# Issuing four follow-up steps of a two-layer gated trunk later in the instruction order

## The chip, the cores and the metric

The kernel runs on 1 core of one Trainium2 chip. The metric is device time in microseconds of one execution of the whole program.

## What is computed

Two layers of a block with two branches over 512 frames of width 1024, in float32. The reference, cut to what the change touches:

```python
for i in range(DEPTH):                                   # 2 layers
    proj = rmsnorm(x, norm1_g[i]) @ w_in[i]
    u_pool, q, k, v, g_a, g_b = split(proj)
    q = apply_partial_rotary(rmsnorm(q, q_norm_g[i]), cos, sin)
    k = apply_partial_rotary(rmsnorm(k, k_norm_g[i]), cos, sin)
    o = diff_attention(q, k, v, lam)                     # 4 heads, two softmaxes each
    attn_out = rmsnorm(o, subln_g[i]) * (1.0 - lam_init)
    pool_out = pool_mixer(u_pool, pool_w[i], pool_scale[i])   # windowed means less u, then a matmul
    merged = sigmoid(g_a) * pool_out + sigmoid(g_b) * attn_out
    x = x + merged @ w_out[i]
    x = x + swiglu(rmsnorm(x, norm2_g[i]))               # hidden width 2816
```

The rotation touches the first 32 of the 128 columns of each q and k. The pool mixer subtracts u from its mean over the last 2, 4, 8 or 16 frames, one window for each of four groups of 256 columns.

## The kernel before

**Products.** Every operand of a matmul is split into a high part, rounded to the matmul's type, and a low part, the rest (`split`, L216: ScalarE writes the high part, VectorE the low one). Each product is then three matmuls: high by high, high by low and low by high. One step of `product` (L302 to L314) is three matmuls of up to 512 columns each, 1536 columns in all.

**Heads.** A layer goes through its four heads in the order 3, 2, 1, 0 (`ORDER`). For head j, `attention` first projects q and k of four token tiles of 128 frames, eight steps each. `evicted` (L625) reads a finished tile out of PSUM: squares and their sums on ScalarE (L629), mean and power on VectorE and POOL (`rsqrt_mean`, L355 and L356). `normed` (L632) scales the tile by the result (four L634 on ScalarE), rotates it (`rotate`: three products L385 and a sum L393 on VectorE), and calls `turned`. That transposes 32 by 32 blocks on VectorE (L326), writes them to DRAM and reads them back in another order (L327 and four L331, issued by SP). In the first head of layer 0 TensorE transposes instead. `turn` then splits the result into qh and ql; `scores` multiplies, takes the row maximum (L550) and the exponential (L551); `joined` combines the two softmaxes; `turn_prob` splits the probabilities (ah, al); `weighted` multiplies by v and `gated` scales the result (L599); `turn_out` writes it into `mj`.

**Branches of the head before.** Between the projections of q and k and that of v, `between` calls `branches` for the head before. It makes two products for the pool mixer, each followed by `windowed` (L697), and two for the gates, each followed by a product with the rows of 1/rms (L731) and a tanh (L732). `windowed` scales the sums (L702), adds up 1 to 4 times with growing shifts (L707), subtracts u (L711, L713) and rounds the result into uh and ul (`split` in L714). `merged` later multiplies uh and ul by the pool weights and merges with the gates and `mj`.

**The order of issue.** The program is unrolled. A counter `clock` adds up the columns of the matmuls issued so far. `later(delay, what)` puts a piece of work on a heap, due that many columns on; `after` does the same, or runs it at once for a delay of 0. `run_due`, called ahead of every step of a product, issues all that is due. `need` issues what is on the heap, in order of due time, until the keys that it is given are in `ready`. From this order of issue the framework builds a queue for each engine. `NORMED` (4800) is the delay from `evicted` to `normed`, `QK_AWAY` (28000) that from `evicted` to `turn`.

**Buffers.** Tiles with one tag share a ring. The ring "qn" has three buffers and holds the tiles of `evicted` and their transposed copies; "us" has two, used by `windowed`; "ta" (the gates) two; the PSUM ring "mm" six and "sc" (scores) two.

Of the kernel before, what the change touches and what calls it, by code (L numbers as in the profile page):

```python
# [13 lines left out]
AF = mybir.ActivationFunctionType  # L14
# [8 lines left out]
NT = S // P  # L23
# [30 lines left out]
SCORE_WAIT, PROB_WAIT, AV_WAIT, NORM_WAIT, MERGE_WAIT = 33600, 25200, 11400, 15000, 15000  # L54

QK_AWAY, SCORE_AWAY, PROB_AWAY, AV_AWAY, MERGE_AWAY = 28000, 26000, 32000, 18000, 24000
NORMED, JOINED, GATED = 4800, 2400, 4800
HIDDEN_DELAYS = (26000, 28000), (8000, 14000)


# [64 lines left out]
def trunk_kernel(  # L125
# [10 lines left out]
    nc = tc.nc  # L136
# [5 lines left out]
    def mm_ps():  # L142
        return ps.tile([P, 512], F32, name="mm", tag="mm", bufs=6)
# [10 lines left out]
    scale = const.tile([P, 3 * L * KD + 4 * L], F32, name="scale")  # L154
# [20 lines left out]
    def gain_column(layer, i):  # L175
        k = 3 * L * KD + 4 * layer + i
        return scale[:, k:k + 1]
# [36 lines left out]
    def split(hi, lo, src):  # L214

        return nc.scalar.copy(hi, src), nc.vector.tensor_sub(lo, src, hi.bitcast(F32))  # L216
# [37 lines left out]
    def wblock(n):  # L254

        return [pair for _ in range(n // 2) for pair in piece()]
# [7 lines left out]
    def later(delay, what):  # L264
        heapq.heappush(waiting, (clock[0] + delay, count[0], what))
        count[0] += 1

    def after(delay, what):
        if delay:
            later(delay, what)  # L270
        else:
            what()

    def run_due(done=None):

        if running[0]:
            return
        running[0] = True
        while waiting and (waiting[0][0] <= clock[0] if done is None else not done()):
            heapq.heappop(waiting)[2]()  # L280
        running[0] = False
        assert done is None or done()
# [34 lines left out]
    def transpose(dst, src):  # L317
        nc.tensor.transpose(dst, src, ident)
        clock[0] += 2 * P
# [25 lines left out]
    def squares_of(x):  # L345
        return x.rearrange("p k (q j) -> p k q j", q=4)

    def rsqrt_mean(ss, n, width, times=(1.0,), eps=None):

        r = sb.tile([P, width], F32, name="r", tag="r", bufs=4)  # L350
        part = width // len(times)
        for i, f in enumerate(times):
            cs = slice(i * part, (i + 1) * part)
            e = EPS / (f * f) if eps is None else eps[i]
            nc.vector.tensor_scalar(r[:, cs], ss[:, cs], 1.0 / (n * f * f), e, op0=ALU.mult, op1=ALU.add)  # L355
        nc.gpsimd.tensor_tensor(r, r, mhalf[:, :width], op=ALU.pow)  # L356
        return r

    def small(name, width=1):
        return sb.tile([P, width], F32, name=name, tag=name, bufs=4)  # L360

    ready = set()

    def need(*keys):
        run_due(lambda: all(k in ready for k in keys))
# [9 lines left out]
    def pair(name, tag, n):  # L375
        return [sb.tile([P, n, S], F32R, name=name + part, tag=tag, bufs=2) for part in "hl"]

    def rotate(qn, t, layer):

        cs, sn = rotary[layer]  # L380
        both = sb.tile([P, 4, 4, ROT], F32, name="m12", tag="m12")

        def by(to, x, table):
            to, x = (v.rearrange("p (a h) r -> p a h r", a=2) for v in (to, x))
            nc.vector.tensor_mul(to, x, table.unsqueeze(2).broadcast_to(list(x.shape)))  # L385

        m1, m2 = both[:, 0], both[:, 1]
        by(m1, qn[:, :, :ROT], cs[:, :, t, :])
        for a in range(2):
            b = (1 - a) * HALF  # L390
            here = slice(a * HALF, (a + 1) * HALF)
            by(m2[:, :, here], qn[:, :, b:b + HALF], sn[:, :, t, here])
        nc.vector.tensor_add(qn[:, :, :ROT], m1, m2)  # L393

    def token(t):
        return slice(t * P, (t + 1) * P)
# [102 lines left out]
    for layer in range(L):  # L499
# [14 lines left out]
        def attention(j, before, then, between):  # L514
# [3 lines left out]
            at_start = not layer and j == ORDER[0]  # L518
# [3 lines left out]
            mj = sb.tile([P, 2, S], F32, name="mj", tag="mj", bufs=2)  # L522
# [4 lines left out]
            def turn(t, qn):  # L527
                if at_start:
                    tp = tr_ps()
                    for h in range(4):  # L530
                        transpose(tp[:, h * P:(h + 1) * P], qn[:, h, :])
                    into, src = [x[:, :, token(t)] for x in (qh, ql)], tp.rearrange("p (h c) -> p h c", h=4)
                else:
                    into, src = [squares_of(x[:, :, token(t)]) for x in (qh, ql)], qn
                nc.scalar.activation(src[:, :2], src[:, :2], AF.Copy, scale=gain_column(layer, 0))
                split(*into, src)
                later(SCORE_WAIT if at_start else SCORE_AWAY, lambda: scores(t))
# [87 lines left out]
            def evicted(t, acc):  # L625
                qn = sb.tile([P, 4, QK], F32, name="qn", tag="qn", bufs=3)
                ss = small("ss4", 4)
                for h in range(4):
                    nc.scalar.activation(qn[:, h, :], acc[:, h * QK:(h + 1) * QK], AF.Square, accum_out=ss[:, h:h + 1])  # L629
                r = rsqrt_mean(ss, QK, 4, (QK ** -0.5, 1.0), [stats[0][:, i, t:t + 1] for i in (3, 4)])  # L630

                def normed():  # L632
                    for h in range(4):
                        nc.scalar.activation(qn[:, h, :], acc[:, h * QK:(h + 1) * QK], AF.Copy, scale=r[:, h:h + 1])  # L634
                    rotate(qn, t, layer)
                    tag = ("us", 2) if roomy and t % 2 else ("qn", 3)
                    near = qn if at_start else turned(qn.rearrange("p h c -> p (h c)"), 4, *tag)
                    later((17400 + 5700 * t if at_start else QK_AWAY) - NORMED, lambda: turn(t, near))

                after(NORMED, normed)  # L640

# [55 lines left out]
        def windowed(j, c, acc, uh, ul):  # L697

            window = WINDOWS[j]
            up = sb.tile([P, 16 + S], F32, name="up", tag="up", bufs=2)  # L700
            nc.vector.memset(up[:, :16], 0.0)
            nc.vector.tensor_mul(up[:, 16:], acc, rms_rows[layer])  # L702
            prev, step, n = up, 1, 0
            while step < window:
                cur = sb.tile([P, 16 + S], F32, name="us", tag="us", bufs=2)
                nc.vector.memset(cur[:, :16], 0.0)
                nc.vector.tensor_add(cur[:, 16:], prev[:, 16:], prev[:, 16 - step:16 + S - step])  # L707
                prev, step, n = cur, step * 2, n + 1
            head = sb.tile([P, 16], F32, name="head", tag="head", bufs=2)
            nc.vector.tensor_mul(head, prev[:, 16:32], inv_t[:, j, :])  # L710
            nc.vector.scalar_tensor_tensor(  # L711
                prev[:, 32:], prev[:, 32:], 1.0 / window, up[:, 32:], op0=ALU.mult, op1=ALU.subtract)
            nc.vector.tensor_sub(prev[:, 16:32], head, up[:, 16:32])  # L713
            split(uh[:, c, :], ul[:, c, :], prev[:, 16:])  # L714

        def branches(j):

            w = wblock(KD)
            pw = pool_weights(j)
            uh, ul = pair("u", "u", 2)  # L720
            for c in range(2):
                acc = mm_ps()
                product(acc, list(zip(cut(w, c * P, (c + 1) * P), x_all())))
                windowed(j, c, acc, uh, ul)

            gates = []
            for c in range(2):
                acc = mm_ps()
                product(acc, list(zip(cut(w, VD + c * P, VD + (c + 1) * P), x_all())))
                ta = sb.tile([P, S], F32, name="ta", tag="ta", bufs=2)  # L730
                nc.vector.tensor_mul(ta, acc, rms_rows[layer])  # L731
                nc.scalar.activation(ta, ta, AF.Tanh, scale=0.5)  # L732
                gates.append(ta)
            return pw, uh, ul, gates

        def merged(j, mj, mh, ml, pw, uh, ul, gates):

            need(*((layer, j, "mj", t) for t in range(NT)))
            for c in range(2):
                y = mm_ps()  # L740
                product(y, list(zip(cut(pw, c * P, (c + 1) * P), [(uh[:, a, :], ul[:, a, :]) for a in range(2)])))
                ta = gates[c]
                k = KD * layer + 2 * j + c
                nc.vector.scalar_tensor_tensor(ta, ta, 1.0, y, op0=ALU.add, op1=ALU.mult)
                nc.vector.scalar_tensor_tensor(ta, ta, scale[:, k:k + 1], mj[:, c, :], op0=ALU.mult, op1=ALU.add)
                split_half(mh[:, c, :], ml[:, c, :], ta)
# [344 lines left out]
```

## Time and profile before

| | us |
|---|---|
| median of 3 runs | 1392.46 (1391.98 to 1392.59) |
| the profiled execution | 1390.53 |
| its span, first to last instruction | 1388.8 |

In the rows of the profile, L634 is line 634 of the kernel. A row of a timeline has the start, the duration, the engine, the line, the operation, and the tile written and those read; in brackets the idle time of the engine just before it and what ended it. A row of the waits has the waiting engine, tile and line, then the engine, tile and line that it waited for, then us in total, how often, and the longest. A row of a stage has for TensorE's matmuls (PE), its weight loads (PEld), VectorE (DVE), ScalarE (ACT) and GpSimd (POOL) the busy time and the number of instructions, then the mean granted TensorE clock, the DMA engines' share, and GB/s. A row of groups has the number of instructions, then the busy time in us and the mean ns of one, then the idle time ahead of them and what ended it. SPq and POOLq are the queues that issue DMAs.

### The profile page before, as it was taken

Reading aid. Unit: us, or ns where it says so; the run is one execution under the profiler, and the core shown is the slowest. Engines: PE = TensorE matmul, PEld = TensorE weight load, DVE = VectorE, ACT = ScalarE, POOL = GpSimd, SP = SyncE. Lnnn points to the kernel's source line nnn. Section 1 sums busy time; section 2 is a strip of 40 time slices with the busy share of each in tenths; the row PEclk is TensorE's granted clock in tenths of the full one; section 3 lists DMA queues with packets and bytes.
Section 4 is the critical chain, followed back from the end, with each engine's and each line's share of the span. In section 5 each row is a group of like instructions: output and inputs, shape, how many; then the busy total and the mean of one; then the engine's idle time right before and its main releaser. Section 6 shows DMA issues by size and latency. Waiting matters only on the chain.

```text
span 1388.8 us, 18685 instructions
## 1 busy us (share of the span) xinstructions
PE 1375.8 (99%) x6242; PEld 1139.1 (82%) x6242; DVE 996.9 (72%) x1787; ACT 776.3 (56%) x1577; POOL 124.5 (9%) x155
## 2 busy tenths in 40 slices
PE   9999999999999999999999899999999999999999
PEld 6888888888888888888888778888888888888887
DVE  7677686766968768578666866867668687686782
ACT  7665555554757545554367555455557565555540
POOL 3010101000101001110010100010001011001100
PEclk9999999999999999999999999999999999999999
DMA  8343453435668968686434354444446688687731
GB/s 309 99 126 114 142 173 123 145 106 167 127 185 198 227 188 226 162 203 199 135 105 159 120 161 139 147 132 139 132 137 152 184 198 233 182 218 176 200 127 61
DMA packets 141072, 224.07 MB, mean 161 GB/s; under 512 B 41392, under 2 KB 88496, under 8 KB 140976
## 3 DMA queue, kind: packets, MB, share of 16 engines
q1 hardware_dynamic: 130464, 187.20, 42.4%
q0 software_dynamic: 9216, 33.56, 14.1%
q10 hardware_dynamic: 1296, 2.13, 0.5%
q8 instruction: 49, 0.80, 0.2%
q14 instruction: 47, 0.39, 0.1%
HBM read 193.59 MB, written 29.23 MB: 160 GB/s over the span
## 4 chain that ended last, share of the span: by engine, by line
PE 94%; DVE 2%; DMA 1%; issue 1%; ACT 1%; SPq 1%; POOL 0%; DVEq 0%; ACTq 0%; POOLq 0%
PE mm L293 14%; PE mm L294 14%; PE mm L292 14%; PE mm L311 13%; PE mm L313 13%; PE mm L312 13%; PE sc L292 3%; PE sc L294 3%; PE sc L293 3%; PE sc L311 1%; PE sc L313 1%; PE sc L312 1%; SPq L331 1%; DVE wlo L216 0%; DMA raw<-in_wts 0%
## 5 line engine op out<-in xcount | busy, mean ns | idle before, releaser
L216 DVE TENSOR_TENSOR wlo<-raw,whi 128x1024 fp32r<-128x1024 f32 (+1 forms) x221 | 267.1, 1214 | 72.0 <-ACT whi L216 71.3
L216 ACT CAST whi<-raw 128x1024 fp32r<-128x1024 f32 (+1 forms) x221 | 230.4, 1048 | 142.4 <-PE mm L294 60.8
L311 PE MATMUL mm<-whi,xh 128*128 128x512 f32 x480 | 188.9, 394 | 0.0
L313 PE MATMUL mm<-whi,xl 128*128 128x512 f32 x480 | 187.4, 390 | 0.0
L312 PE MATMUL mm<-wlo,xh 128*128 128x512 f32 x480 | 187.2, 390 | 0.0
L292 PE MATMUL mm<-fh,whi 128*128 128x512 f32 (+1 forms) x356 | 137.7, 387 | 0.0
L294 PE MATMUL mm<-fh,wlo 128*128 128x512 f32 (+1 forms) x356 | 137.7, 387 | 0.0
L293 PE MATMUL mm<-fl,whi 128*128 128x512 f32 (+1 forms) x356 | 137.7, 387 | 0.0
L749 DVE TENSOR_TENSOR res<-mm,res 128x512 f32<-128x512 f32 (+1 forms) x145 | 97.9, 679 | 45.0 <-PE mm L294 41.8
L313 PEld LDWEIGHTS mm<-whi,xl 128*128 128x128 f32 x480 | 90.1, 188 | 18.6
L312 PEld LDWEIGHTS mm<-wlo,xh 128*128 128x128 f32 x480 | 90.3, 188 | 17.1
L311 PEld LDWEIGHTS mm<-whi,xh 128*128 128x128 f32 x480 | 90.3, 188 | 16.8
L242 POOL DMA_DIRECT2D wlo<-in_wts x64 | 56.1, 876 | 530.7 <-ACT wlo L241 359.0
L356 POOL TENSOR_TENSOR r<-r,mhalf 128x4 f32<-128x4 f32 (+1 forms) x64 | 52.5, 822 | 536.6 <-DVE r L355 536.6
L311 PE MATMUL mm<-xh,whi 128*128 128x512 f32 x256 | 100.3, 392 | 0.0
L313 PE MATMUL mm<-xh,wlo 128*128 128x512 f32 x256 | 100.3, 392 | 0.0
L312 PE MATMUL mm<-xl,whi 128*128 128x512 f32 x256 | 100.1, 391 | 0.0
L292 PE MATMUL mm<-whi,xh 128*128 128x512 f32 x224 | 87.2, 389 | 0.0
L294 PE MATMUL mm<-whi,xl 128*128 128x512 f32 x224 | 87.2, 389 | 0.0
L293 PE MATMUL mm<-wlo,xh 128*128 128x512 f32 x224 | 87.2, 389 | 0.0
L241 ACT ACTIVATE wlo<-raw 128x1024 fp32r<-128x1024 f32 x64 | 67.7, 1058 | 29.0 <-PE mm L293 27.9
L293 PEld LDWEIGHTS mm<-fl,whi 128*128 128x128 f32 x356 | 66.9, 188 | 13.6
(232 smaller groups left out, 2966.6 us busy)
## 6 DMA issues: line engine op xcount, KB each, us to landing
raw<-in_wts SPq DMA_DIRECT2D x243, 512.0 KB, 4.0
wlo<-in_wts POOLq DMA_DIRECT2D x64, 512.0 KB, 6.4
away<-near SPq DMA_DIRECT2D x73, 256.0 KB, 2.3
near<-away SPq DMA_DIRECT2D x292, 64.0 KB, 2.9
away<-near SPq DMA_DIRECT2D x29, 128.0 KB, 1.7
near<-away SPq DMA_DIRECT2D x116, 32.0 KB, 2.1
pwr<-in_pool_w ACTq DMA_DIRECT2D x8, 256.0 KB, 4.7
out<-res SPq DMA_DIRECT2D x7, 256.0 KB, 2.0
```

Source lines behind the costliest of these rows:

```text
L216: return nc.scalar.copy(hi, src), nc.vector.tensor_sub(lo, src, hi.bitcast(F32))
L241: made[0] = nc.scalar.activation(lo, raw, AF.Copy, scale=-1.0)
L242: nc.gpsimd.dma_start(lo.rearrange("p a b -> p (a b)"), wts[piece_no], accum_op=ALU.add)
L292: nc.tensor.matmul(acc, lhsT=ah, rhs=bh, start=start, stop=False, **check)
L293: nc.tensor.matmul(acc, lhsT=ah, rhs=bl, start=False, stop=False, **check)
L294: last = nc.tensor.matmul(acc, lhsT=al, rhs=bh, start=False, stop=stop, **check)
L311: nc.tensor.matmul(acc, lhsT=ah, rhs=bh, start=i == 0, stop=False)
L312: nc.tensor.matmul(acc, lhsT=ah, rhs=bl, start=False, stop=False)
L313: last = nc.tensor.matmul(acc, lhsT=al, rhs=bh, start=False, stop=i == n - 1)
L331: nc.sync.dma_start(near[32 * c:32 * (c + 1), :].rearrange("i (q r) -> i q r", q=4), away.rearrange("(q i) (c r) -> c i q r", q=4, c=4)[c])
L356: nc.gpsimd.tensor_tensor(r, r, mhalf[:, :width], op=ALU.pow)
L749: return nc.vector.tensor_add(res[d][:, cs], acc, res[d][:, cs])
```

## The change

`normed` is cut in two: the scaling is due after 7200 columns instead of 4800, and the rotation with all that follows it 2400 columns after the scaling. The delay to `turn` is shortened by as much, so that it stays at 28000 columns from `evicted`. In `windowed`, the rounding into uh and ul is due 9600 columns later. In `branches`, the tanh of a gate is due 2400 columns later. `merged` now also needs both roundings and both tanhs to have been issued.

```diff
-NORMED, JOINED, GATED = 4800, 2400, 4800
+NORMED, ROTATED, JOINED, GATED, SUMMED, GATE = 7200, 2400, 2400, 4800, 9600, 2400
...
                 def normed():
                     for h in range(4):
                         nc.scalar.activation(qn[:, h, :], acc[:, h * QK:(h + 1) * QK], AF.Copy, scale=r[:, h:h + 1])
+                    after(ROTATED, rotated)
+
+                def rotated():
                     rotate(qn, t, layer)
                     tag = ("us", 2) if roomy and t % 2 else ("qn", 3)
                     near = qn if at_start else turned(qn.rearrange("p h c -> p (h c)"), 4, *tag)
-                    later((17400 + 5700 * t if at_start else QK_AWAY) - NORMED, lambda: turn(t, near))
+                    later((17400 + 5700 * t if at_start else QK_AWAY) - NORMED - ROTATED, lambda: turn(t, near))
...
-            split(uh[:, c, :], ul[:, c, :], prev[:, 16:])
+
+            def rounded():
+                split(uh[:, c, :], ul[:, c, :], prev[:, 16:])
+                ready.add((layer, j, "u", c))
+
+            after(SUMMED, rounded)
...
-                nc.scalar.activation(ta, ta, AF.Tanh, scale=0.5)
                 gates.append(ta)
+
+                def bent(c=c, ta=ta):
+                    nc.scalar.activation(ta, ta, AF.Tanh, scale=0.5)
+                    ready.add((layer, j, "g", c))
+
+                after(GATE, bent)
...
-            need(*((layer, j, "mj", t) for t in range(NT)))
+            need(*((layer, j, "mj", t) for t in range(NT)), *((layer, j, x, c) for x in "ug" for c in range(2)))
```

## The prediction, made before the changed kernel had run

> **What bounds the kernel now.** I read the page's first part, then who waited for whom on TensorE, then the stages in which TensorE fell short, and there the timelines of the engines.
>
> ```profile
> PE 1375.8 (99%) x6242; PEld 1139.1 (82%) x6242; DVE 996.9 (72%) x1787; ACT 776.3 (56%) x1577; POOL 124.5 (9%) x155
> PE sc L311 <- ACT pr L551: 4.2, 1, 4.2
> PE mm L311 <- ACT ah L216: 2.4, 1, 2.4
> ...
> 780.00:800.00 20.00, 15.79 (x68) 12.85 (x67) 18.29 (x55) 9.48 (x22) 0.54 (x1) 0.91 0.34 92
> 800.00:820.00 20.00, 18.07 (x84) 14.77 (x82) 11.45 (x31) 10.18 (x32) 1.32 (x2) 1.00 0.57 188
> ```
>
> TensorE works in 99% of the span. Moving work on ScalarE and VectorE can pay only where TensorE waits for them, and apart from the start there are two such places, both early in layer 1: 4.21 us at 781.8 for an exponential, and 2.44 us at 818 for the rounded probabilities of a token tile. The mean clock of 0.91 in the first of these windows says that the stall costs more than its idle time.
>
> ```profile
> 780.54 0.39 PE L311 MATMUL mm<-xh,whi 128*128 128x512 f32 x1
> ...
> 781.22 0.39 PE L311 MATMUL mm<-xh,whi 128*128 128x512 f32 x1
> ...
> 786.05 0.58 PE L311 MATMUL sc<-qh 128*128 128x256 f32 x1 [4.21 <-ACT pr L551]
> ...
> 786.86 0.63 PE L313 MATMUL mm<-xh,wlo 128*128 128x512 f32 x1
> 787.29 0.63 PE L311 MATMUL mm<-xh,whi 128*128 128x512 f32 x1
> ...
> 788.97 0.28 PE L311 MATMUL sc<-qh 128*128 128x256 f32 x1
> ```
>
> Three matmuls of 512 columns, one step of a product, take 0.68 us (780.54 to 781.22), so 0.227 us each. After the stall they start 0.43 us apart. From 786.05 to 788.97 stand three matmuls of 256 columns and five of 512; at full speed that is 3 x 0.113 + 5 x 0.227 = 1.47 us, and it took 2.92. So the stall costs 4.21 + 1.45 = 5.7 us, and the second one 2.4 with no slow matmuls behind it.
>
> Behind the first stall stands a chain of engines that wait in order:
>
> ```profile
> 759.28 0.71 DVE L326 STREAM_TRANSPOSE near<-qn 128x512 f32<-128x512 f32 x1
> 759.92 0.17 DVE L355 TENSOR_SCALAR r<-sso,rc 128x1 f32<-128x1 f32 x1
> 760.75 0.48 DVE L599 SCALAR_TENSOR_TENSOR mt<-mm,r,tb 128x256 f32<-128x256 f32 x1 [0.66 <-POOL r L356]
> ...
> 762.54 0.48 DVE L599 SCALAR_TENSOR_TENSOR mt<-mm,r,tb 128x256 f32<-128x256 f32 x1 [0.73 <-POOL r L356]
> ...
> 763.77 0.32 DVE L355 TENSOR_SCALAR r<-ss,stats 128x2 f32<-128x2 f32 x2
> 766.12 1.14 ACT L634 ACTIVATE qn<-mm,r 128x128 f32<-128x128 f32 x4 [2.04 <-POOL r L356]
> ...
> 768.43 2.03 ACT L216 CAST whi<-raw 128x1024 fp32r<-128x1024 f32 x2
> 770.33 0.53 ACT L535 ACTIVATE near<-near,scale 128x256 f32<-128x256 f32 x1
> ...
> 774.20 0.28 ACT L629 ACTIVATE qn<-mm 128x128 f32<-128x128 f32 x1 [2.68 <-DVE near L326]
> ...
> 776.80 0.37 ACT L634 ACTIVATE qn<-mm,r 128x128 f32<-128x128 f32 x1 [1.07 <-POOL r L356]
> 777.07 0.61 ACT L216 CAST qh<-near 128x512 fp32r<-128x512 f32 x1
> 778.32 0.69 DVE L702 TENSOR_TENSOR up<-mm,hg 128x512 f32<-128x512 f32 x1
> 784.82 0.17 DVE L713 TENSOR_TENSOR us<-head,up 128x16 f32<-128x16 f32 x1
> 784.91 0.28 DVE L550 TENSOR_REDUCE mx<-sc 128x1 f32<-128x128 f32 x1
> 785.02 0.62 ACT L216 CAST uh<-us 128x512 fp32r<-128x512 f32 x1 [4.90 <-DVE us L713]
> 785.55 0.36 ACT L551 ACTIVATE pr<-sc,mx 128x128 f32<-128x128 f32 x1
> ```
>
> Read it from below. The exponential at 785.55 frees the bank that TensorE wants. It follows the rounding of the pool sums (785.02) on ScalarE and the row maximum (784.91) on VectorE, which stands behind the whole pool chain (L702 at 778.32 to L713). That chain starts late because q and k of earlier tiles were late: ScalarE waited 1.07 us for the power on POOL (776.80), and before that 2.68 us (774.20) for a free qn buffer, which hangs on the transposes and round trips of tiles 0 to 2, and these on VectorE's two waits for POOL (0.66 and 0.73).
>
> **What the change does to the queues.** The delays are in columns of the issue order, and one row shows that an engine's queue does not follow that order strictly:
>
> ```profile
> 726.69 0.07 DVE L706 MEMSET us<- 128x16 f32 x1
> ```
>
> This memset is issued after L702, yet it ran 51.6 us ahead of the layer's first L702 (778.32). The queues are put together at build time: an instruction thought ready goes ahead, and issue order decides only between instructions that are ready together. A delay is therefore lost priority, not lost time. Hence, part by part:
>
> ```profile
> L634 ACT ACTIVATE qn<-mm,r 128x128 f32<-128x128 f32 x120 | 34.8, 371 | 29.4 <-POOL r L356 29.4
> L216 ACT CAST uh<-us 128x512 fp32r<-128x512 f32 x16 | 9.9, 621 | 38.2 <-DVE us L713 32.5 <-DVE us L706 5.7
> L732 ACT ACTIVATE ta<-ta 128x512 f32<-128x512 f32 x16 | 10.1, 628 | 12.5 <-DVE ta L731 9.4 <-DVE us L706 3.0
> ```
>
> - **Instructions added or removed: none.** The sum of work stays.
> - **Scaling by 1/rms (L634)**: due after 4800 columns, so issued after 4 steps (work is issued at steps of 1536); now 7200, 5 steps: 0.68 us of priority. It waits for POOL with ScalarE idle beside it (29.4 us over 120 rows). An idle engine takes it whatever its priority, so that wait stays. I cost it at 0; bounds: if ScalarE did put other ready work ahead, minus 29.4/32 = 0.9 us for a tile, or plus 0.68.
> - **Rotation (three L385, L393, the transpose L326, and SP's one outward and four return transfers)**: from step 4 to step 7, so 2.04 us. The due time of the later `turn` is 6144 + 23200 = 29344 columns before and 10752 + 18400 = 29152 after: the same step, or the one before.
> - **Rounding of the sums (uh, then ul)**: 9600 columns, 7 steps or 4.8 us, still within the next product (8 steps) and thus before `windowed` runs again on the two `us` buffers. At 785.02 uh was ready 0.17 us before the maximum was done on an idle ScalarE, so it will still go first; the most to gain is 785.55 less 785.19, 0.36 us. I take 0. ul gives way to the second maximum on VectorE, which TensorE does not wait for.
> - **Tanh of the gates**: 2 steps, 1.4 us; its product follows a whole v projection later, except in a layer's last head, where `need` issues it at once. 0, at most one row of 0.63 us.
>
> The part that can matter is the rotation in layer 1's second head. There the weighted sums of the head before (TensorE's first row of them is at 757.12) are issued where the rotation used to be:
>
> ```profile
> 757.12 0.28 PE L311 MATMUL mm<-vh,ah 128*128 128x256 f32 x1
> ...
> 767.26 0.39 PE L313 MATMUL mm<-whi,xl 128*128 128x512 f32 x1
> 756.14 1.01 POOL L356 TENSOR_TENSOR r<-r,mhalf 128x4 f32<-128x4 f32 x1 [4.06 <-DVE r L355]
> ...
> 760.17 0.55 POOL L356 TENSOR_TENSOR r<-r,mhalf 128x1 f32<-128x1 f32 x1 [3.02 <-DVE r L355]
> 764.23 1.85 POOL L356 TENSOR_TENSOR r<-r,mhalf 128x4 f32<-128x4 f32 x1 [1.72 <-DVE r L355]
> 764.00 1.22 DVE L216 TENSOR_TENSOR wlo<-raw,whi 128x1024 fp32r<-128x1024 f32 x1
> ```
>
> With the rotation three steps later, the two short L355 (0.17 us) of those sums win over the transpose of 0.71 us at 759.28, and POOL's 0.55 us then runs beneath the transpose. VectorE's waits of 0.66 and 0.73 us go: 1.39 us. The next L355 pair moves from 763.77 to 762.4 and pulls L634 (766.12) with it. Next comes the pair of weight casts at 768.43. TensorE frees the last buffer of the projection near 767.65 (its last row starts at 767.26), and TensorE does not move: if the first cast waits for that, 0.8 us of the gain is left, if neither does, all 1.39. I take 1.1 and carry it through to the exponential. The stall then is 4.21 - 1.1 = 3.1 us.
>
> Does the clock still fall to half? The trace shows it falling after 4.21 us and not after 2.44. The estimate of 3.1 is nearer to 2.44, so I take no fall: 1.45 us more. [...]
>
> The POOL row of 1.85 us stands against 1.01 for the same form (756.14) and lies beneath a VectorE instruction with two inputs (764.00). The pair moved to 762.4 would miss it, and up to 0.8 us more might come; I leave that out, since the casts hold the chain next. [...]
>
> **Sum.** Against the profiled execution, 1390.53 us (span 1388.8 and 1.7 around it): -1.1 - 1.45 = -2.55, so 1388.0. It lies 1.93 us below the median of the runs, 1392.46; on that scale the forecast is 1389.9. Its own range is 1388.5 to 1391.4 (gain 1.1 with the clock still falling, or 1.39 and a little at the second stall).
>
> **Rivals.**
> - **The change does nothing that can be measured**: the engines are idle where the moved work stands, and the queues come out the same. For it: ScalarE's idle 4.90 us ahead of uh, the idle waits of L634. Against it: VectorE is busy for 18.29 of 20 us around the stall, and there priority does decide. 1392.4.
> - **The first stall goes altogether**, if the maximum gets ahead of the pool chain: -4.21 - 1.45 = -5.7, 1386.8. For it: that tile's scores were done before the stall began, and the maximum waits for VectorE's turn alone. Against it: L702 to L713 keep their places in the issue order, only the rounding behind them leaves.
> - **Slower: the ring of three qn buffers.** If the queues do follow the later rotation, each transposed tile comes back 2.04 us later, the 2.68 us wait for a qn buffer at 774.20 grows by as much, and both stalls with it: +4.1, 1396.5. It decides once a transpose lies later than its round trip has room for:
>
> ```profile
> 755.77 8.42 SPq L327 DMA_DIRECT2D away<-near  x4
> 764.29 8.00 SPq L331 DMA_DIRECT2D near<-away  x16
> away<-near SPq DMA_DIRECT2D x73, 256.0 KB, 2.3
> ```
>
> Tile 0's outward transfer was issued at 755.77 and landed some 2.3 us later; its return was issued at 764.29, behind three outward transfers that waited for VectorE. That leaves 6.2 us of room for tile 0, which speaks against this rival; tile 2, whose transpose ends the wait at 774.20, has none.
>
> **How the numbers follow.** About 0.2%, 2.8 us, is what a measurement of this kernel can tell from no change. Forecast 0.40, nothing 0.25, stall gone 0.20, slower 0.15. A third of the forecast's case lies beyond 0.2%: faster 0.33, same 0.54 (the rest of it, the second case, and a little of the fourth), slower 0.13. The range runs from below the third case to half way into the fourth, 1386.3 to 1394.3.
>
> **What would show it.** Right: in layer 1's second head the L355 of the weighted sums ahead of the rotation's transpose, VectorE's two waits for POOL gone, the TensorE wait for pr near 3 us and a clock of 1.00 behind it; the 29.4 us of L634 for POOL hardly changed. Wrong: the same order on VectorE from 758 to 785 (nothing changes), L550 ahead of L702 (third case), or a wait of L629 for near above 2.68 us and stalls above 4.21 and 2.44 (fourth).

## The result and the profile after

| | before | after |
|---|---|---|
| median, us | 1392.53 (1391.98 to 1393.56, 4 runs) | 1400.83 (1400.15 to 1401.62, 4 runs) |
| span of the profiled execution, us | 1388.8 | 1398.4 |

The ratio after to before is 1.0059, with a 95% interval of 1.0042 to 1.0076: 8.3 us slower by the medians. The forecast was 1389.9 with a range up to 1394.3. The time lies above the range, and even the slower rival (1396.5) fell short of it.

The waits of TensorE come first again. A row has the waiting engine, tile and line, what it waited for, us in total, how often, and the longest. Rows of the kernel after:

```profile
PE sc L311 <- ACT pr L551: 3.8, 3, 2.6
PE mm L311 <- ACT ah L216: 2.3, 2, 2.0
PE mm L311 <- ACT vh L682: 2.3, 4, 0.6
PE sc L311 <- ACT qh L216: 2.1, 2, 1.1
PE mm L312 <- DVE vl L683: 1.6, 5, 0.3
PE sc L312 <- DVE ql L216: 1.3, 2, 0.7
```

The first two rows were there before (4.2 and 2.4, once each): the wait for pr now comes three times. The other four are new but for one of the five waits for vl. Those for vh and vl stand in heads 1 and 0 of both layers, hence fours, and those for qh and ql (which hold q and k) in head 1 of both, hence pairs. TensorE had no wait there before. The stages of the kernel after show where the time now goes. The fields are: stretch, then its length, then for PE, PEld, DVE, ACT and POOL busy time and number of instructions, then the granted clock, the DMA share and GB/s.

```profile
200.00:220.00 20.00, 17.73 (x72) 13.65 (x72) 12.12 (x25) 9.72 (x25) 1.04 (x2) 0.91 0.47 146
780.00:800.00 20.00, 16.78 (x80) 13.67 (x79) 16.42 (x55) 9.91 (x35) 1.56 (x2) 1.00 0.45 135
```

The first of these stretches in the kernel before:

```profile
200.00:220.00 20.00, 20.00 (x96) 16.45 (x95) 10.99 (x23) 8.30 (x23) 1.10 (x2) 1.00 0.47 143
```

The stretch from 780, which the whole prediction was about, has in fact become better (16.78 us busy at a full clock, against 15.79 at 0.91). The loss is at 200, in layer 0, in a place where the kernel before worked without a gap. There the timeline of TensorE shows all of it (start, duration, engine, line, operation, tiles, in brackets the idle time ahead of the row and its releaser):

```profile
200.05 0.39 PE L313 MATMUL mm<-whi,xl 128*128 128x512 f32 x1
201.49 0.49 PE L311 MATMUL sc<-qh 128*128 128x512 f32 x1 [1.06 <-ACT qh L216]
202.64 0.57 PE L312 MATMUL sc<-ql,qh 128*128 128x512 f32 x1 [0.65 <-DVE ql L216]
203.01 0.63 PE L313 MATMUL sc<-qh,ql 128*128 128x512 f32 x1
203.44 0.63 PE L311 MATMUL sc<-qh 128*128 128x512 f32 x1
...
206.00 0.56 PE L311 MATMUL mm<-whi,xh 128*128 128x512 f32 x1
...
209.36 0.39 PE L313 MATMUL mm<-whi,xl 128*128 128x512 f32 x1
210.31 0.39 PE L311 MATMUL mm<-vh,ah 128*128 128x256 f32 x1 [0.56 <-ACT vh L682]
```

Three costs stand in these ten microseconds. The scores of tile 3 wait for qh and ql: 200.05 to 201.49 to 202.64 are two starts where 0.23 us each would do, so 2.1 us. Then matmuls start 0.43 us apart instead of 0.23 until 206.00: the granted clock has fallen, to 0.50 from 202.93 to 206.33. And the weighted sum of tile 0 starts 0.95 us behind its forerunner instead of 0.23, because vh isn't there yet; a wait of 0.32 us for vl follows 21 us on, in the weighted sum of tile 3.

**The sum of the two profiled executions.** Per head, the waits for v cost 0.72 us and about 0.5 for vl, 1.2 in each of four heads: 4.8. The waits for q and k cost 2.1 in each of the two heads 1: 4.2. The slow clock behind 202.64 costs 1.7 (one start of 0.37 us, seven of 0.43 and one of 0.39 instead of 0.23). A new wait for pr of 0.60 us in the first head of layer 0, with its restart, costs 0.8. The start of layer 1 gains 2.2: its waits with their restarts and slow matmuls come to 8.7 us before (4.4, 1.45, 2.6 and 0.3) and 6.5 after (2.7, 0.8, 0.3, 2.2 and 0.5). Together 9.3; the spans differ by 9.6.

### The profile page after: what moved, and what is told of

It is laid out like the page before. It is cut to its first block, busy times and chain, and to the rows that moved or that the text cites. A ratio compares the mean times of both kernels' runs of the same rounds, so it can differ in the third digit from the quotient of the medians.

```text
span 1398.4 us, 18671 instructions
## 1 busy us (share of the span) xinstructions
PE 1379.3 (99%) x6242; PEld 1139.3 (81%) x6242; DVE 996.6 (71%) x1787; ACT 775.9 (55%) x1577; POOL 125.7 (9%) x155
## 4 chain that ended last, share of the span: by engine, by line
PE 87%; DVE 5%; DMA 3%; ACT 2%; SPq 2%; issue 1%; POOL 1%; DVEq 0%; ACTq 0%; POOLq 0%
PE mm L292 14%; PE mm L293 14%; PE mm L294 14%; PE mm L311 11%; PE mm L312 11%; PE mm L313 11%; PE sc L292 3%; PE sc L294 3%; PE sc L293 3%; DVE wlo L216 2%; SPq L331 2%; DMA near<-away 1%; DMA away<-near 1%; PE sc L312 1%; DMA away<-pr 1%
## 5 line engine op out<-in xcount | busy, mean ns | idle before, releaser
L294 PEld LDWEIGHTS mm<-fh,wlo 128*128 128x128 f32 x356 | 66.9, 188 | 13.6
```

The lines of the kernel that those rows point to most:

```text
L294: last = nc.tensor.matmul(acc, lhsT=al, rhs=bh, start=False, stop=stop, **check)
```

## What the column counter shows

The delays are counted in columns, and work is issued only between the steps of a product. So I wrote out the counter `clock` at which each piece is issued. For head 1 of layer 0 (the figures of its four token tiles, before and after):

```
            tile 0            tile 1            tile 2            tile 3
rotation    310784  315392    323072  327680    359936  365312    372992  377600
turn        335360  333824    347648  346112    383744  383744    397568  396032
scores      361472  359936    374528  372992    409856  409856    424448  422912
weighted    436736  435200    448256  449792    463616  463616    479744  478208
```

The delay to `turn` was meant to stay at 28000 columns from `evicted`. But it is counted from the step at which the rotation was issued, itself rounded up to a step, and comes out 192 columns shorter in all. That is enough to reach the step before. In heads 1 and 0 of both layers, `turn` of tiles 0, 1 and 3 thus falls one step (1536 columns, 0.68 us) **earlier**, and its scores with it; the weighted sums of tiles 0 and 3 too. (That of tile 1 finds v not ready, looks again 2400 columns on, and ends one step later than before.) In layer 1's first head, too, all four turns come one step earlier; in its second head, the one that the prediction worked on, all four keep their step. So the change, called a delay, also moves work forward. The timeline of TensorE has the same count: between the scores of tile 2 and those of tile 3 stand 24 matmuls before and 21 after.

Three theories follow. **A, the early turn**: scores and weighted sums that come one step early meet operands that aren't ready. **B, the late rotation**: each tile of q and k comes back from DRAM later, and its `turn` with it. **C, rounding and tanh**, the change's other half.

## The experiments

Every ratio is to runs of the kernel before on the same chip. All kernels compute the whole of the reference.

**x1: the change, with `turn` at its old step.** All four delays stay; a mark is set where the scaling stood, and `turn` is counted from there.

```diff
-                    later((17400 + 5700 * t if at_start else QK_AWAY) - NORMED - ROTATED, lambda: turn(t, near))
+                    later((17400 + 5700 * t if at_start else QK_AWAY) - 4800 - (clock[0] - old[0]), lambda: turn(t, near))
...
+                old = []
+                after(4800, lambda: old.append(clock[0]))
```

> All four delays of the change stay, but turn is due at the very step at which it was before the change (a mark at 4800 columns keeps the old clock), so scores, joined, turn_prob and weighted are issued where they were. Theory A (the change's loss comes from turn and all behind it being issued one step earlier, 29152 columns against 29344): about 1391 us, no wait of TensorE for vh or qh left in the later heads, and the shorter stall of layer 1's second head (2.6 us instead of 4.2) kept. Theory B (the rotation's transfers lose their place on SP to those of the probabilities, whatever turn does): 1396 to 1398 us, with the waits of TensorE for qh and ql near 201 and 896 us still there. Theory C (the rounding of the pool sums or the tanh is what comes late): about 1400 us.

Measured: 1391.35 us (1389.81 to 1392.98), ratio 1.0002 (0.9992 to 1.0011). The whole loss is gone with all four delays in place, and TensorE's waits are those of the kernel before again (pr 4.2, ah 2.4; none for q, k or v but the one for vl). One part of theory A's expectation failed: the shorter stall of layer 1's second head is not kept, so the four delays alone do not shorten it.

**x2: the kernel before, with `turn` alone 192 columns earlier**, which is one step in the same heads, and in layer 1's first.

```diff
-                    later((17400 + 5700 * t if at_start else QK_AWAY) - NORMED, lambda: turn(t, near))
+                    later((17400 + 5700 * t if at_start else QK_AWAY) - NORMED - 192, lambda: turn(t, near))
```

> The kernel before, with nothing changed but turn due 192 columns earlier, which puts it and all behind it one step earlier in the heads 1 and 0 of both layers and in the first head of layer 1. Theory A: about 1397 to 1400 us, with the four pairs of waits of TensorE for vh and vl (about 1.2 us a head, 4.9 in all) and those for qh. Theory B: 1397 for the waits for vh and vl alone (4.9 us), none for qh, since the transfers keep their place. Theory C: 1392.5.

Measured: 1397.22 us (1395.44 to 1398.68), ratio 1.0045 (1.003 to 1.006). Rows of its waits:

```profile
PE mm L311 <- ACT vh L679: 2.3, 4, 0.6
PE mm L312 <- DVE vl L680: 1.6, 5, 0.3
```

The waits for v are all there, those for qh and ql are not. Most of the loss needs none of the four delays, only the one step.

**x3: rounding and tanh delayed alone**, scaling, rotation and `turn` as before.

```diff
-NORMED, ROTATED, JOINED, GATED, SUMMED, GATE = 7200, 2400, 2400, 4800, 9600, 2400
+NORMED, ROTATED, JOINED, GATED, SUMMED, GATE = 4800, 0, 2400, 4800, 9600, 2400
```

> The change's rounding of the pool sums and tanh alone; scaling, rotation and turn as before. Theories A and B: 1392 us, within 1 of the kernel before. Theory C: about 1400 us.

Measured: 1392.02 us (1391.0 to 1394.17), ratio 1.0009 (1.0 to 1.0018), the waits as before (4.2 and 2.4). At most 2.5 us, and no wait that would carry it.

**x4: the delays of scaling and rotation alone**, rounding and tanh at once.

```diff
-NORMED, ROTATED, JOINED, GATED, SUMMED, GATE = 7200, 2400, 2400, 4800, 9600, 2400
+NORMED, ROTATED, JOINED, GATED, SUMMED, GATE = 7200, 2400, 2400, 4800, 0, 0
```

> The change's scaling and rotation alone, with turn as the change has it; rounding and tanh as before. Theories A and B: about 1400 us, as the whole change. Theory C: 1392.5 us.

Measured: 1401.47 us (1399.54 to 1403.91), ratio 1.0074 (1.0057 to 1.0092), with the new waits of the kernel after, to a tenth (qh 2.1, ql 1.3, vh 2.3, vl 1.6). The loss belongs to q and k.

**x5: x2, with the weighted sums of heads 1 and 0 back at their old steps.** Everything else of x2 stays early.

```diff
+                if j < 2 and not t and ("late", layer, j) not in ready:
+                    ready.add(("late", layer, j))
+                    later(1, lambda: weighted(t, ah, al))
+                    return
...
-                later(AV_WAIT if at_start else AV_AWAY + (4800 if roomy else 0), lambda: weighted(t, ah, al))
+                later(AV_WAIT if at_start else AV_AWAY + (4800 if roomy else 0) + (1536 if j < 2 and t % 2 else 0), lambda: weighted(t, ah, al))
```

> The run with the turn alone one step earlier (x2), but the weighted sums of the heads 1 and 0 go back to the steps that they have in the kernel before; turn, scores, joining and turned probabilities stay one step early. Theory A2 (the weighted sum of tile 0 stands directly behind v's projection of its own tile, 24 matmuls instead of 27, so TensorE waits for vh and then vl, 0.56 and 0.32 us in each of four heads, with their restart about 1.2 us): the vh group falls from 2.3 us to at most 0.2 and the vl group from 1.6 to about 0.3, and the time from 1397.2 to 1392 to 1393. Rival R2 (the earlier scores or turned probabilities cost the time, by the engines they find busy, and the waits for v only stand where the time is lost): the waits move to other operands and the time stays at 1396 to 1398.

Measured: 1390.95 us (1390.58 to 1393.7), ratio 1.0003 (0.9993 to 1.0012). The waits for vh are gone, and of those for vl the one is left that the kernel before has. The first rows:

```profile
PE sc L311 <- ACT pr L551: 4.1, 2, 2.7
PE mm L311 <- ACT ah L216: 2.3, 2, 2.0
```

Earlier turns, scores and probabilities cost nothing by themselves; it is the weighted sums that take all of x2's loss. The run moves them together: the waits for vh stand at tile 0, those for vl at tile 3.

**x6 and x7: x2 with one more thing later.** In x6 the rotation comes four steps behind the scaling, which stays (four steps later than before, where the change has three); in x7 scaling and rotation both come one step later. Both keep x2's step of `turn`, and rounding and tanh as before.

```diff
-NORMED, JOINED, GATED = 4800, 2400, 4800
+NORMED, ROTATED, JOINED, GATED, SUMMED, GATE = 4800, 4800, 2400, 4800, 0, 0
```

```diff
-NORMED, JOINED, GATED = 4800, 2400, 4800
+NORMED, ROTATED, JOINED, GATED, SUMMED, GATE = 7200, 0, 2400, 4800, 0, 0
```

> The run x2 with one thing moved: the rotation of q and k is issued 4 steps (2.7 us) behind the scaling, as in the kernel after, while the scaling stays where it is before, and rounding and tanh too. Theory B (the rotation's round trip on SP then stands behind that of the probabilities of the tile before, turn of tile 3 comes some 12 us late, TensorE waits for qh and ql in head 1 of each layer): the groups qh near 2.1 us and ql near 1.3 us as in the kernel after, the trip of the fourth tile issued right behind that of the probabilities near 187 us, and 1400 to 1402. Rival (the qh wait of the kernel after needs the later scaling, or rounding and tanh): no qh wait, 1397.

> The run x2 with scaling and rotation together one step (0.68 us) later, the rotation directly behind the scaling; rounding and tanh as before. Theory B: one step isn't enough for the rotation's trip to fall behind the probabilities' on SP (in the kernel before it is issued 5 us ahead of them), so no qh wait and about 1397. Rival (the later scaling makes qh late): qh 2.1 us, ql 1.3 us and 1400 to 1402.

Measured: x6 1401.19 us (1398.54 to 1404.18), ratio 1.007 (1.0051 to 1.0088), with qh 2.1 and ql 1.3; x7 1397.56 us (1395.07 to 1398.56), ratio 1.004 (1.0025 to 1.0056), with no wait for qh. So the later rotation, and not the later scaling, makes q and k late. SP's queue in x6 shows how it begins:

```profile
185.96 0.36 SPq L327 DMA_DIRECT2D away<-pr  x1
186.37 0.43 SPq L327 DMA_DIRECT2D away<-near  x1
```

The outward transfer of tile 3 (`near`) now stands behind that of the probabilities of tile 1 (`pr`), and its returns behind theirs. In x7 they still go first:

```profile
183.54 0.38 SPq L327 DMA_DIRECT2D away<-near  x1
184.03 0.36 SPq L327 DMA_DIRECT2D away<-pr  x1
```

That is not the whole of it, as x1 shows. There too SP sends the probabilities first, and yet nothing waits:

```profile
183.80 0.34 SPq L327 DMA_DIRECT2D away<-pr  x1
184.18 0.43 SPq L327 DMA_DIRECT2D away<-near  x1
```

The difference lies on ScalarE, first in x1, then in the kernel after. L535 begins the `turn` of tile 3, L551 is the exponential of tile 2:

```profile
195.55 0.50 ACT L535 ACTIVATE near<-near,scale 128x256 f32<-128x256 f32 x1
196.25 0.58 ACT L551 ACTIVATE pr<-sc,mx 128x384 f32<-128x384 f32 x1 [0.20 <-DVE mx L550]
...
196.82 0.61 ACT L216 CAST qh<-near 128x512 fp32r<-128x512 f32 x1
```

```profile
199.30 0.58 ACT L551 ACTIVATE pr<-sc,mx 128x384 f32<-128x384 f32 x1 [1.04 <-DVE mx L550]
...
199.88 0.50 ACT L535 ACTIVATE near<-near,scale 128x256 f32<-128x256 f32 x1
200.28 0.57 ACT L551 ACTIVATE pr<-sc,mx 128x384 f32<-128x384 f32 x1
...
200.83 0.61 ACT L216 CAST qh<-near 128x512 fp32r<-128x512 f32 x1
```

In the kernel after, the `turn` stands in ScalarE's queue behind an exponential that sits idle for VectorE's maximum (1.04 us), and qh behind a second one. In x1 the `turn` has its place ahead of both exponentials, and qh ahead of the second (198.28). The framework builds the queue from the order of issue, so I take it that the later return in the plan cost the `turn` its place; what the builder weighed can't be read from a trace, and no run moved the `turn` on ScalarE alone.

**x11: the kernel after, with the weighted sums back at their old steps** (x5's edit on it), to see whether the two costs add up.

> The kernel after with one thing undone: the weighted sums of heads 1 and 0 go back to the steps that they have in the kernel before (x5's edit put on the kernel after). Theory (two costs that add up: the weighted sum of tile 0 one step early behind v, and the turn of tile 3 late against its scores): the vh group falls from 2.3 us to 0.6 or less and the vl group to about 0.3, the qh 2.1 and ql 1.3 stay, and of the 8 to 9 us some 4.8 go: a ratio to before of about 1.003, 1394.5 to 1396. Rival (the q waits push the weighted sums, or what is saved is lost at the next wait): the ratio stays above 1.005.

Measured: 1396.05 us (1394.82 to 1399.19), ratio 1.0034 (1.0022 to 1.0047). The waits for vh are gone, those for q and k stay:

```profile
PE sc L311 <- ACT qh L216: 2.1, 2, 1.1
```

The costs are separate, and the waits for v are worth 1398.4 - 1393.7 = 4.7 us between the two spans (mean granted clock 0.999 and 0.998), for the 4.8 worked out above. The two ratios, from different batches of runs, differ by less, 1.0059 against 1.0034 or 3.5 us, and their intervals overlap.

**x8, x9 and x10: can the first stall of layer 1 be taken away?** The third case of the prediction was that the maximum L550 gets ahead of the pool sums. x8 issues the scores of tile 0 of that head one step earlier, ahead of the sums:

```diff
-                later(SCORE_WAIT if at_start else SCORE_AWAY, lambda: scores(t))
+                later(SCORE_WAIT if at_start else SCORE_AWAY - (800 if layer and j == ORDER[1] and not t else 0), lambda: scores(t))
```

x9 cuts the sums themselves into pieces in `windowed`, each at least 1500 columns behind the last, only in the branch of layer 1's first head, which runs beside the second head's products (for all others `following` calls at once); x10 is both.

```diff
-            while step < window:
-                cur = sb.tile([P, 16 + S], F32, name="us", tag="us", bufs=2)
...
+            def sums(prev, step):
+                if step < window:
+                    cur = sb.tile([P, 16 + S], F32, name="us", tag="us", bufs=2)
...
+                    following(lambda: sums(cur, step * 2))
+                    return
...
+            def following(do):
+                if layer and j == ORDER[0]:
+                    later(1500, do)
+                else:
+                    do()
```

> The kernel before with one step of it moved: the scores of tile 0 in the second head of layer 1 are issued one step earlier, ahead of the running pool sums of that head instead of behind. Theory (the first stall of layer 1, 4.21 us for pr, comes from the maximum L550, which stands on VectorE behind the chain of pool sums): the chain then follows the maximum, the wait for pr falls below 1 us, no clock fall behind it, and 1386 to 1388 against 1391 to 1392. Rival (VectorE's backlog is what is late; what goes first there pushes what follows): the wait moves to another operand behind the pool sums and the time stays within 1.5 us of the kernel before.

> The kernel before with the running pool sums of layer 1's first pool branch (about 7 us of VectorE at a stretch, twice) issued in pieces, each at least 1500 columns behind the last, so that maxima and transposes of the head beside it find a place between them. Theory (the first stall of layer 1 is that block of VectorE work, whichever maximum stands behind it): no wait for pr or qh over 1 us near 785, 4 to 5.7 us less with the clock not falling, 1385.5 to 1387.5 against 1391. Rival (VectorE is behind by its total work there): the wait turns up on another operand and the time stays within 1.5 us.

> x9 with the scores of tile 0 in the second head of layer 1 one step earlier as well (x8's edit). Theory: as x9 or up to 1 us less where the first maximum still meets a piece of the sums. Rival: as x9's rival, 1391.

Measured: x8 1391.16 us (ratio 0.9999, 0.999 to 1.0008), x9 1389.9 us (0.9991, 0.9982 to 1.0), x10 1391.35 us (0.9999, 0.999 to 1.0008). In each the wait changed its operand. Rows of x8, then of x9:

```profile
PE sc L311 <- ACT qh L216: 3.5, 1, 3.5
```

```profile
PE mm L311 <- ACT ah L216: 2.7, 2, 2.4
PE sc L311 <- ACT qh L216: 1.9, 1, 1.9
...
PE sc L311 <- ACT pr L551: 1.0, 1, 1.0
```

In x8 the wait for pr is gone and a wait of 3.5 us for qh stands in its place: the next tile's qh lies on ScalarE behind the next exponential, which waits 2.34 us for a maximum that stands among the pool sums again. Slices (x9) save about 1 us of waiting (1.9, 1.0 and 2.7 us against 4.2 and 2.4), and the time follows by as much, but its interval reaches 1.0. None is shown to beat the kernel before.

## Why the prediction was wrong

**The step that failed** is the one on the rotation, where the due time of `turn` was worked out, 29344 columns before and 29152 after, and dismissed as "the same step, or the one before". In layer 1's second head, where the prediction priced everything, it was the same step. In heads 1 and 0 of both layers it was the one before, and that was never priced. Rows of the kernel before would have given the price. ScalarE, then TensorE:

```profile
205.40 0.47 ACT L679 ACTIVATE vh<-mm,stats 128x256 fp32r<-128x256 f32 x1 [4.41 <-PE mm L313]
```

```profile
205.65 0.39 PE L313 MATMUL mm<-whi,xl 128*128 128x512 f32 x1
205.93 0.39 PE L311 MATMUL mm<-vh,ah 128*128 128x256 f32 x1
```

vh is done at 205.87, and the weighted sum that reads it starts at 205.93. There is no idle time in that place, but only 0.06 us to spare. One step earlier is 0.68 us, so a wait of 0.62 was to be expected in each head; 0.56 was measured. The vl of tile 3 is done at 226.45 (225.98 and 0.47 more, on VectorE) and read at 226.71, which leaves 0.26 us: a wait of 0.42 was to be expected, and 0.32 was measured. Shown by x2 (the step alone: 1.0045), x5 (the weighted sums back: 1.0003) and x1 (all four delays without the step: 1.0002).

**Behind it stood a reading of the waits** that was too simple: "apart from the start there are two such places" where moving work on ScalarE and VectorE can pay. That is right for gains. For losses the question is how much room each operand has, and a table of waits lists only those that have run out of it.

**The slower rival had the right mechanism in the wrong place.** It said that a later rotation brings each tile back later, and looked for the harm in the ring of qn buffers and the two stalls of layer 1. The tiles do come back later, and TensorE does wait, but in heads 1, for qh and ql, by way of a queue and not a buffer. The wait of L629 for the buffer became smaller (its longest in that head is 1.86 us in the kernel after, 2.68 before; it grew to 2.86 in x6, whose rotation is later still, but with no longer stall of TensorE behind it). x6 shows the later rotation's part: 2.1 and 1.3 us of waits that x2 doesn't have. Its ratio is 1.007 against x2's 1.0045, but from different batches of runs, and the intervals overlap. But x1, with the rotation as late and `turn` at its old step, lost nothing: the rotation costs only together with the early step.

**"A delay is lost priority, not lost time"** held as long as `turn` kept its step: all four delays together cost nothing (x1), nor could a cost of rounding and tanh alone be told from none (x3). The idle time ahead of the scaling's 120 rows for POOL, which the forecast had as hardly changing from 29.4 us, did not change in x1 (29.4) and rose to 37.2 in the kernel after.

**The first stall** did shrink, from 4.21 us to 2.56 and 0.66, and the clock behind it stayed at 1.00: 3.2 us in all, for the 3.1 of the forecast. The number was right by accident. Rows of VectorE, kernel after:

```profile
765.72 0.20 DVE L355 TENSOR_SCALAR r<-sso,rc 128x1 f32<-128x1 f32 x1
...
766.58 0.48 DVE L599 SCALAR_TENSOR_TENSOR mt<-mm,r,tb 128x256 f32<-128x256 f32 x1 [0.46 <-POOL r L356]
...
767.81 0.17 DVE L355 TENSOR_SCALAR r<-sso,rc 128x1 f32<-128x1 f32 x1
767.90 0.70 DVE L326 STREAM_TRANSPOSE near<-qn 128x512 f32<-128x512 f32 x1
...
785.22 0.68 DVE L705 TENSOR_TENSOR up<-mm,hg 128x512 f32<-128x512 f32 x1
...
789.99 0.28 DVE L550 TENSOR_REDUCE mx<-sc 128x1 f32<-128x128 f32 x1
...
790.27 0.67 DVE L714 SCALAR_TENSOR_TENSOR us<-us,up 128x496 f32<-128x496 f32 x1
```

The two L355 did overtake the transpose (767.90), and the two waits for POOL fell from 1.39 us to 0.46, as forecast. But the later rotation alone does not bring this about. In x1, with all four delays, the transpose is still ahead, and the two waits are 0.67 and 0.73 us:

```profile
758.27 0.71 DVE L326 STREAM_TRANSPOSE near<-qn 128x512 f32<-128x512 f32 x1
758.91 0.17 DVE L355 TENSOR_SCALAR r<-sso,rc 128x1 f32<-128x1 f32 x1
```

Nor did the pool sums come 1.1 us earlier: they begin 3.0 us ahead of the stall (785.22 against 788.26) and began 3.5 ahead of it before (778.32 against 781.84). What broke the stall in two is that the maximum at 789.99 now stands ahead of the end of the pool sums (L714 and what follows it), which the prediction had made a case of its own. The early `turn` does that by itself. TensorE in x2 (x5 has the same, 2.73 and 1.39):

```profile
786.46 0.39 PE L311 MATMUL sc<-qh 128*128 128x256 f32 x1 [2.73 <-ACT pr L551]
788.48 0.58 PE L311 MATMUL sc<-qh 128*128 128x256 f32 x1 [1.40 <-ACT pr L551]
```

So it is the early `turn` of layer 1's first head, where the forecast saw the late rotation of the second. But these two waits make 4.1 us, as much as the one of 4.2 before. Less is waited in all only where scaling and rotation are delayed as in the change and `turn` is early too: 3.2 us in the kernel after and in x11, 2.8 in x4. How the two act together there, no run takes apart.

**The clock** was where the forecast's reading came apart. The forecast took no fall for a wait of about 3 us, and there it didn't fall. That was luck: in x1 a clock of 0.50 from 820.29 to 823.69 followed the wait for ah, with 2.4 us as long as the one behind which the clock of the kernel before had held. In the kernel after it fell at 202.9, behind two waits of 1.06 and 0.65 us that the forecast didn't have, and that cost 1.7 us.

## What to carry to other kernels

A delay counted from a point that is itself rounded to a step moves what follows it by a whole step, either way: write out the step at which every piece is issued, before and after, ahead of pricing anything. A place without a wait can have 0.06 us to spare: for each piece that comes earlier, compare the end of its last operand with its start in the trace. And a late transfer can cost more than its lateness, if what needs it is placed in its engine's queue behind other work that waits for something else, as `turn` was here behind an exponential that waited 1.04 us.

## What the runs showed of the hardware

In these runs the clock didn't fall behind long waits alone. The stretches below were cut at the places where the granted clock changes; the field behind POOL is the clock. First x1, then the kernel after:

```profile
786.16:789.56 3.40, 3.40 (x11) 2.72 (x11) 3.40 (x14) 1.31 (x3) 0.00 (x0) 0.50 0.65 198
...
816.87:820.27 3.40, 0.96 (x5) 0.33 (x3) 1.01 (x2) 1.76 (x4) 0.00 (x0) 1.00 0.58 190
820.29:823.69 3.40, 3.33 (x11) 2.99 (x12) 0.23 (x2) 0.47 (x2) 0.55 (x1) 0.50 0.34 80
```

```profile
199.52:202.92 3.40, 1.69 (x7) 0.88 (x6) 3.26 (x7) 3.40 (x9) 0.00 (x0) 1.00 0.78 206
202.93:206.33 3.40, 3.40 (x9) 2.65 (x9) 3.25 (x8) 1.10 (x2) 0.00 (x0) 0.50 0.54 140
```

Each of these falls lasts 3.4 us, as does the one of the kernel before (785.51 to 788.92), and the two of x1 begin 34.13 us apart. In x2 the mean clock from 780 to 800 was 0.83, by my estimate from that figure 6.8 us at 0.50. TensorE was idle for 72% of the 3.40 us ahead of x1's second fall (0.96 us busy) and for half of the 3.40 us ahead of the fall at 202.9 (1.69 busy), though no single wait there was longer than 1.06 us. So the prediction's reading by the length of a single stall, a fall behind 4.21 us and none behind 2.44, does not hold here: 0.50 followed a wait of 2.4 us in x1, and waits of 1.06 and 0.65 us in the kernel after.

The wait of x1 lies whole in the 3.40 us ahead of its fall. In the kernel before, the wait of 2.44 us brought no fall; TensorE was busy for 1.83 and 2.46 us of the two stretches of 3.41 us below, across which it lies, and the clock was 1.00 in both:

```profile
816.23:819.64 3.41, 1.83 (x9) 1.18 (x7) 1.66 (x4) 0.95 (x3) 0.30 (x1) 1.00 0.58 196
819.64:823.05 3.41, 2.46 (x14) 2.08 (x15) 0.77 (x2) 1.28 (x4) 0.00 (x0) 1.00 0.42 112
```

What sets the two cases apart is not shown: no run here set out to move a wait.
